# Block inverses of a gated delta rule on TensorE: the order of the 32x32 products, and the 64-block steps of two directions in one function

## Chip, cores and metric

The kernel runs on one core of a Trainium2 chip. The metric is device time in microseconds (us) of one execution. A profiled execution gives the rows below; its own time lies a little above the timed ones.

## What is computed

A two-layer encoder trunk over 256 tokens of width 1024. Each layer has a SwiGLU block, a mixer with two branches (a bidirectional gated delta rule and a multi-head latent attention), and a second SwiGLU block. The change lies in the delta rule of the mixer. Of the reference, this is the part:

```
unit = jnp.eye(C, dtype=f32) + lower                # lower: strictly triangular, C = 64
uw = lax.linalg.triangular_solve(unit, rhs, left_side=True, lower=True, unit_diagonal=True)
...
o_fwd = gated_delta_chunked(qh, kh, vh, g[:, :, 0], beta[:, :, 0])
o_bwd = flip(gated_delta_chunked(flip(qh), flip(kh), flip(vh), flip(g[:, :, 1]), flip(beta[:, :, 1])))
```

The kernel works on chunks of 128 tokens. Instead of solving, it forms the inverse of each 128x128 triangular matrix: two directions (d = 0, 1), two chunks (t) and four heads (h), so eight matrices n = (t, h) for each direction and layer.

## The kernel before

The inverse is built up by blocks. `gdn_base` makes the inverses of all 16x16 diagonal blocks by a recursion on GpSimd. Then come three doublings, each of two product steps: `inv0` and `inv1` go from 16 to 32, `inv2` and `inv3` from 32 to 64, `inv4` and `inv5` from 64 to 128. A step multiplies an off-diagonal block of `LA` (or a result `t1s` of the step before) by an inverse made so far (`XC`, `ZC`, its transpose, `x64` for the 64-blocks, `Z` for the whole). All of these are float32 in SBUF; one partition range of 32 or 64 rows holds one block row, so each product uses one 32x32 (or 64x64) place of the 128x128 array, given by the partitions that it reads and the partitions that it writes.

- `inv0(d)` and `inv1(d)` (lines 828 to 846) make 32 products of 32x32 each, in the four places on the diagonal of the array: the outer loop runs over the four places `Q`, the inner one over the eight matrices, so eight products in a row use one place. `inv0` is evicted by ScalarE (L834), `inv1` by VectorE (L841), which also transposes (L843) and copies into `Z` (L845).
- `inv2(d)` (L848 to L864) makes 16 products in two places, all eight of the first place and then all eight of the second; VectorE and ScalarE evict one half each (L857).
- `inv3(d)` (L866 to L881) makes 16 products `pu` in two places (L872) and then 8 products `px` in a third (L876).
- `inv4(d)` and `inv5(d)` (L883 to L896) make 8 products of 64x64 each, in one place for d = 0 and in another for d = 1.

The results go to PSUM tiles `gd`, of which there are two in turn. In the profile a float32 product is two pairs of a weight load and a matmul, so the 32 products of an `inv0` are x64 there. Below, a pair is one of these.

The steps are called in the order that the end of `mixer` lists (L1016 to L1037), but a scheduler then sets each engine's order by its own estimate of times, so that dense products of other parts (`qkv_group` L550, the gates and projections L141 to L143, the attention heads L644, L657, L674, L686) stand between the steps. Each engine works its list in order. Five bursts of 32x32 products result in each layer, each followed by other products: `inv0(0)`; `inv1(0)` with `inv0(1)`; `inv2(0)` with `inv1(1)`; `inv3(0)` with `inv2(1)`; and `inv3(1)`. They hold 64, 128, 96, 80 and 48 pairs.

Of the kernel before, what the change touches and what calls it, by code (L numbers as in the profile page):

```python
# [20 lines left out]
P = 128  # L21
# [16 lines left out]
def encoder_trunk(ctx: ExitStack, tc: tile.TileContext, x, positions, norm_ffn1, ffn1_w_gate, ffn1_w_up,  # L38
# [4 lines left out]
    V, A, G, T = nc.vector, nc.scalar, nc.gpsimd, nc.tensor  # L43
# [14 lines left out]
    def gdp():  # L58
        return psum.tile([P, 512], F32, tag="gd", name="gd", bufs=2)
# [358 lines left out]
    def mixer(l, next_gain):  # L418
# [7 lines left out]
        with tc.tile_pool(name="mix", bufs=1) as mp:  # L426
            def t2(tag, bufs, shape=(P, NH, P)):
                return mp.tile(list(shape), F32, tag=tag, name=tag, bufs=bufs)

            def g2(shape=(P, NH, P)):  # L430
                return t2("g2", 4, shape)
# [262 lines left out]
            LA, Z, egc, cs = {}, {}, {}, {}  # L694
# [21 lines left out]
            def gdn_nv(nk_):  # L716
                for t in range(NT):
                    pv = gdp()
                    for h in range(NH):
                        T.transpose(out=pv[:, h * P:(h + 1) * P], in_=vT[h // 2][:, h % 2, t * P:(t + 1) * P],  # L720
                                    identity=ident)
                    V.tensor_tensor(out=nV[t], in0=ev4(pv), in1=bc(nk_[:, t, :]), op=ALU.mult)
# [43 lines left out]
            N8 = NT * NH  # L766
# [3 lines left out]
            def flat(ap):  # L770
                return ap.rearrange("p a b -> p (a b)")
# [39 lines left out]
            def ij(d, b, o0):  # L811
                fst, snd = slice(o0, o0 + b), slice(o0 + b, o0 + 2 * b)
                return (snd, fst) if d == 0 else (fst, snd)

            def blocks(ps, c0, b):
                return ps[:, c0:c0 + N8 * b].rearrange("p (n d) -> p n d", d=b)

            TH = [(t, h) for t in range(NT) for h in range(NH)]
            Q = [slice(q * 32, q * 32 + 32) for q in range(4)]

            t1s, x64 = {}, {}
# [5 lines left out]

            def inv0(d):
                pv = blocks(gdp(), 0, 32)
                for r in Q:  # L830
                    for n, (t, h) in enumerate(TH):
                        T.matmul(pv[r, n], lhsT=LA[d, t][r, h, 1, r], rhs=XC[r, d, n], start=True, stop=True)
                t1s[d] = t2("t1", 4, (P, N8, 32))
                A.copy(out=t1s[d], in_=pv)  # L834

            def inv1(d):
                pv = blocks(gdp(), 0, 32)
                for r in Q:
                    for n in range(N8):
                        T.matmul(pv[r, n], lhsT=ZC[r, d, n], rhs=t1s[d][r, n], start=True, stop=True)  # L840
                V.copy_predicated(out=XC[:, d], mask=(mlo if d == 0 else mup)[:, None, :].to_broadcast([P, N8, 32]),  # L841
                                  data=pv)
                V.transpose(out=flat(ZC[:, d]), in_=flat(XC[:, d]))  # L843
                for q, r in enumerate(Q):
                    (A.copy if q % 2 else V.tensor_copy)(  # L845
                        out=Z[d][r, :, :, r].rearrange("p t h a -> p (t h) a"), in_=ZC[r, d])

            def inv2(d):  # L848
                pv = blocks(gdp(), 0, 32)
                t1s[d] = t2("t1", 4, (P, N8, 32))  # L850
                for o0 in (0, 64):
                    I, J = ij(d, 32, o0)
                    for n, (t, h) in enumerate(TH):
                        T.matmul(pv[I, n], lhsT=LA[d, t][J, h, 1, I], rhs=XC[J, d, n], start=True, stop=True)
                for o0 in (0, 64):
                    I, J = ij(d, 32, o0)
                    (A.copy if o0 else V.tensor_copy)(out=t1s[d][I], in_=pv[I])  # L857

                x64[d] = g2((P, N8, 64))
                o = 64 * d  # L860
                G.memset(x64[d][o:o + 64], 0.0)
                for k in range(2):
                    G.tensor_copy(out=x64[d][o + 32 * k:o + 32 * k + 32, :, 32 * k:32 * k + 32],
                                  in_=XC[o + 32 * k:o + 32 * k + 32, d])  # L864

            def inv3(d):  # L866
                ps = gdp()
                pu, px = blocks(ps, 0, 32), blocks(ps, N8 * 32, 32)
                for o0 in (0, 64):
                    I, J = ij(d, 32, o0)  # L870
                    for n, (t, h) in enumerate(TH):
                        T.matmul(pu[J, n], lhsT=t1s[d][I, n], rhs=ZC[I, d, n], start=True, stop=True)  # L872
                o = 64 * d
                I, J = ij(d, 32, o)
                for n in range(N8):
                    T.matmul(px[I, n], lhsT=ZC[I, d, n], rhs=t1s[d][I, n], start=True, stop=True)  # L876
                A.copy(out=x64[d][I, :, J.start - o:J.stop - o], in_=px[I])
                for o0 in (0, 64):
                    I, J = ij(d, 32, o0)
                    (A.copy if o0 else V.tensor_copy)(  # L880
                        out=Z[d][J, :, :, I].rearrange("p t h a -> p (t h) a"), in_=pu[J])  # L881

            def inv4(d):  # L883
                I, J = ij(d, 64, 0)
                pv = blocks(gdp(), 0, 64)
                t1s[d] = g2((P, N8, 64))
                for n, (t, h) in enumerate(TH):
                    T.matmul(pv[I, n], lhsT=LA[d, t][J, h, 1, I], rhs=x64[d][J, n], start=True, stop=True)
                (A.copy if d else V.tensor_copy)(out=t1s[d][I], in_=pv[I])

            def inv5(d):
                I, J = ij(d, 64, 0)
                pv = blocks(gdp(), 0, 64)
                for n, (t, h) in enumerate(TH):
                    T.matmul(pv[J, n], lhsT=t1s[d][I, n], rhs=Z[d][I, t, h, I], start=True, stop=True)
                (A.copy if d else V.tensor_copy)(out=Z[d][J, :, :, I].rearrange("p t h a -> p (t h) a"), in_=pv[J])  # L896

            zz, qs = {}, {}

# [115 lines left out]
            dense(xh, xl, NKC, wl_, C_Z, 512, ev_z)  # L1015
            inv_zero()  # L1016
            inv0(0)
            inv1(0)
            inv0(1)
            inv2(0)  # L1020
            inv1(1)
            m1 = mla_dense(1)
            gb = [gate(C_G + D)]
            gb.append(gate(C_G + D + 512))
            inv3(0)
            at0(0)
            inv2(1)
            at0(1)
            inv4(0)
            inv3(1)  # L1030
            inv4(1)
            qkv_group(4)
            qkv_group(5)
            gdn_nv(nk_)
            inv5(0)
            at1 = mla_heads(*m1)
            inv5(1)  # L1037
            sts = {}
            sts[0] = gdn_first(0)
            at1(0)  # L1040
# [34 lines left out]
    for l in range(depth):  # L1075
        ffn(ffn1_w_gate[l], ffn1_w_up[l], ffn1_w_down[l], G_MX + 8 * l, mixer_consts if l == 0 else None)
        mixer(l, G_F2 + 8 * l)
        ffn(ffn2_w_gate[l], ffn2_w_up[l], ffn2_w_down[l], G_F1 + 8 * (l + 1) if l + 1 < depth else None)
# [26 lines left out]
```

## Time and profile before

| | us |
|---|---|
| median of three timed runs | 1253.03 (1252.57 to 1253.27) |
| the profiled execution's own time | 1257.24 |
| span of the profiled execution | 1255.5 |
| TensorE busy in it | 1225.0 |
| VectorE busy | 774.5 |
| ScalarE busy | 624.1 |
| GpSimd busy | 132.7 |

The span runs from the first to the last instruction; about 1.7 us of the execution lie around it. The mixers' inverses lie at about 312 to 366 us in the first layer and 932 to 986 us in the second. In rows, PE is TensorE's matmuls, PEld its weight loads, DVE is VectorE, ACT ScalarE, POOL GpSimd, SP the engine that issues DMAs; L832 is line 832 of the kernel. Ends of matmuls are modelled, and overlap with the next starts, so what a piece takes on the path is read from its start to the next piece's start.

### The profile page before, as it was taken

Reading aid. Unit: us, or ns where it says so; the run is one execution under the profiler, and the core shown is the slowest. Engines: PE = TensorE matmul, PEld = TensorE weight load, DVE = VectorE, ACT = ScalarE, POOL = GpSimd, SP = SyncE. Lnnn points to the kernel's source line nnn. Section 1 sums busy time; section 2 is a strip of 40 time slices with the busy share of each in tenths; the row PEclk is TensorE's granted clock in tenths of the full one; section 3 lists DMA queues with packets and bytes.
Section 4 is the critical chain, followed back from the end, with each engine's and each line's share of the span. In section 5 each row is a group of like instructions: output and inputs, shape, how many; then the busy total and the mean of one; then the engine's idle time right before and its main releaser. Section 6 shows DMA issues by size and latency. Waiting matters only on the chain.

```text
span 1255.5 us, 17613 instructions
## 1 busy us (share of the span) xinstructions
PE 1225.0 (98%) x7064; PEld 1036.0 (83%) x7064; DVE 774.5 (62%) x1127; ACT 624.1 (50%) x911; POOL 132.7 (11%) x238
## 2 busy tenths in 40 slices
PE   8999999899999999999999999998999999999997
PEld 6888889777988888888888888897778788888886
DVE  5655557986757665555555554588876576555554
ACT  6554446556445455453454444465554455544443
POOL 1000001445001000000000000015540000000010
PEclk9999999999899999999999999998999999999999
DMA  7564555435232555555555555543452235565652
GB/s 266 176 198 149 204 185 158 154 120 168 69 101 81 173 183 175 194 168 196 192 183 187 182 169 207 178 147 121 144 162 75 68 134 185 168 201 169 200 185 84
DMA packets 114576, 202.70 MB, mean 161 GB/s; under 512 B 4107, under 2 KB 30399, under 8 KB 114495
## 3 DMA queue, kind: packets, MB, share of 16 engines
q1 hardware_dynamic: 114031, 200.52, 49.1%
q8 instruction: 55, 0.90, 0.3%
q10 hardware_dynamic: 464, 1.06, 0.2%
q14 instruction: 26, 0.21, 0.0%
HBM read 200.52 MB, written 1.05 MB: 161 GB/s over the span
## 4 chain that ended last, share of the span: by engine, by line
PE 88%; DVE 4%; POOL 4%; issue 1%; ACT 1%; DMA 0%; POOLq 0%; SPq 0%; ACTq 0%
PE acc L141 24%; PE acc L142 23%; PE acc L143 23%; PE acc L550 4%; PE ms L191 2%; DVE wlo L131 2%; POOL bt L798 1%; PE ms L686 1%; PE ms L657 1%; POOL t L800 1%; PE gd L141 1%; PE gd L142 1%; PE gd L143 1%; PE gd L927 1%; DVE cv L566 1%
## 5 line engine op out<-in xcount | busy, mean ns | idle before, releaser
L131 DVE TENSOR_TENSOR wlo<-raw,whi 128x1024 fp32r<-128x1024 f32 (+3 forms) x388 | 471.4, 1218 | 364.2 <-ACT whi L130 362.0
L130 ACT CAST whi<-raw 128x1024 fp32r<-128x1024 f32 (+3 forms) x388 | 399.7, 1033 | 429.4 <-PE acc L143 384.9
L142 PE MATMUL acc<-wlo,xh 128*128 128x512 f32 (+3 forms) x968 | 360.7, 374 | 0.0
L143 PE MATMUL acc<-whi,xl 128*128 128x512 f32 (+3 forms) x968 | 357.5, 372 | 0.0
L141 PE MATMUL acc<-whi,xh 128*128 128x512 f32 (+3 forms) x968 | 344.7, 375 | 0.1
L142 PEld LDWEIGHTS acc<-wlo,xh 128*128 128x128 f32 x968 | 182.4, 188 | 29.8 <-issue 0.4
L141 PEld LDWEIGHTS acc<-whi,xh 128*128 128x128 f32 x968 | 181.4, 188 | 30.3 <-ACT xh L115 0.8
L143 PEld LDWEIGHTS acc<-whi,xl 128*128 128x128 f32 x968 | 182.1, 188 | 29.2
L142 PE MATMUL acc<-wlo,hh 128*128 128x512 f32 x352 | 137.4, 390 | 0.0
L143 PE MATMUL acc<-whi,hl 128*128 128x512 f32 x352 | 137.1, 389 | 0.0
L141 PE MATMUL acc<-whi,hh 128*128 128x512 f32 x352 | 127.4, 392 | 0.0
L143 PEld LDWEIGHTS acc<-whi,hl 128*128 128x128 f32 x352 | 66.1, 188 | 13.8
L141 PEld LDWEIGHTS acc<-whi,hh 128*128 128x128 f32 x352 | 66.1, 188 | 13.7
L142 PEld LDWEIGHTS acc<-wlo,hh 128*128 128x128 f32 x352 | 66.1, 188 | 13.1
L141 PE MATMUL acc<-whi,fr 128*128 128x512 f32 (+1 forms) x152 | 60.7, 406 | 9.2 <-DVE pre L558 7.9
L142 PE MATMUL acc<-wlo,fr 128*128 128x512 f32 (+1 forms) x152 | 60.8, 402 | 0.0
L143 PE MATMUL acc<-whi,fr 128*128 128x512 f32 (+1 forms) x152 | 58.0, 399 | 2.4 <-DVE fr L116 2.4
L550 PE MATMUL acc<-xl,whi 128*128 128x256 f32 x192 | 56.9, 297 | 0.0
L550 PE MATMUL acc<-xh,whi 128*128 128x256 f32 x192 | 56.9, 298 | 0.0
L550 PE MATMUL acc<-xh,wlo 128*128 128x256 f32 x192 | 54.8, 296 | 0.0
L566 DVE SCALAR_TENSOR_TENSOR cv<-pre,ccol,cv 128x256 f32<-128x256 f32 x96 | 51.9, 572 | 0.0
L255 ACT ACTIVATE sil<-acc,rstd 128x512 f32<-128x512 f32 (+1 forms) x48 | 31.0, 654 | 29.5 <-PE acc L143 29.4
(299 smaller groups left out, 1277.7 us busy)
## 6 DMA issues: line engine op xcount, KB each, us to landing
raw<-in_ffn_w_up_dram SPq DMA_DIRECT2D x40, 1024.0 KB, 5.0
raw<-in_ffn_w_down_dram SPq DMA_DIRECT2D x40, 1024.0 KB, 5.0
raw<-in_ffn_w_gate_dram SPq DMA_DIRECT2D x38, 1024.0 KB, 5.0
raw<-in_w_in_dram SPq DMA_DIRECT2D x32, 1024.0 KB, 4.9
raw<-in_w_out_dram SPq DMA_DIRECT2D x8, 1024.0 KB, 4.9
raw<-in_ffn_w_gate_dram SPq DMA_DIRECT2D x12, 512.0 KB, 3.7
raw<-in_ffn_w_up_dram SPq DMA_DIRECT2D x8, 512.0 KB, 3.7
raw<-in_ffn_w_down_dram SPq DMA_DIRECT2D x8, 512.0 KB, 3.3
```

The source lines that it names most:

```text
L130: A.copy(out=hi[:, :n * w], in_=raw[:, k0 * w:(k0 + n) * w])
L131: V.tensor_tensor(out=lo[:, :n * w], in0=raw[:, k0 * w:(k0 + n) * w], in1=hi[:, :n * w].bitcast(F32), op=ALU.subtract)
L141: T.matmul(ps[t][:, :n], lhsT=a1, rhs=w[0], start=start, stop=False)
L142: T.matmul(ps[t][:, :n], lhsT=a1, rhs=w[1], start=False, stop=False)
L143: T.matmul(ps[t][:, :n], lhsT=a2, rhs=w[0], start=False, stop=stop)
L191: T.transpose(out=pt[:, i * S + t * P:i * S + (t + 1) * P], in_=srcs[t][:, (j + i) * P:(j + i + 1) * P], identity=ident)
L255: A.activation(out=sil[t][:, :w], in_=ps, func=AF.Silu, scale=rstds[0][:, t:t + 1])
L550: T.matmul(pc[:, c].rearrange("p (t s) -> p t s", s=P), lhsT=w[:, cc], rhs=a, start=(i == 0), stop=(i == len(terms) - 1))
L566: V.scalar_tensor_tensor(out=cv[:, c], in0=pre[:, c, d:d + S], scalar=wc, in1=cv[:, c], op0=ALU.mult, op1=ALU.add)
L657: T.matmul(sc[:, t * S:(t + 1) * S], lhsT=qT[:, t * P:(t + 1) * P], rhs=kT, start=True, stop=True)
L686: T.matmul(po[r:r + MV, :S], lhsT=v[:, kk, h, :], rhs=prT[:, kk, :], start=(kk == 0), stop=(kk == NT - 1))
L798: G.tensor_tensor(out=tv, in0=M[:, b + 1:16, b:b + 1].to_broadcast([P, na, nb]), in1=Y[:, b:b + 1, 0:nb].to_broadcast([P, na, nb]), op=ALU ...
```

## The change

`inv0` and `inv1` swap their loops: for each matrix, the four places in turn. `inv2` does so with its two places. `inv3` makes, for each matrix, the two `pu` products and then the `px` product. `inv4` and `inv5` lose their argument: one call makes both directions, direction by direction for each matrix, into two `gd` tiles taken at once, and is called after `inv3(1)`, and after `gdn_nv`, respectively. No product, copy or DMA is added or dropped.

```
             def inv0(d):
                 pv = blocks(gdp(), 0, 32)
-                for r in Q:
-                    for n, (t, h) in enumerate(TH):
+                for n, (t, h) in enumerate(TH):
+                    for r in Q:
                         T.matmul(pv[r, n], lhsT=LA[d, t][r, h, 1, r], rhs=XC[r, d, n], start=True, stop=True)
...
             def inv1(d):
-                for r in Q:
-                    for n in range(N8):
+                for n in range(N8):
+                    for r in Q:
                         T.matmul(pv[r, n], lhsT=ZC[r, d, n], rhs=t1s[d][r, n], start=True, stop=True)
...
             def inv2(d):
-                for o0 in (0, 64):
-                    I, J = ij(d, 32, o0)
-                    for n, (t, h) in enumerate(TH):
+                for n, (t, h) in enumerate(TH):
+                    for o0 in (0, 64):
+                        I, J = ij(d, 32, o0)
                         T.matmul(pv[I, n], lhsT=LA[d, t][J, h, 1, I], rhs=XC[J, d, n], start=True, stop=True)
...
             def inv3(d):
-                for o0 in (0, 64):
-                    I, J = ij(d, 32, o0)
-                    for n, (t, h) in enumerate(TH):
+                o = 64 * d
+                for n in range(N8):
+                    for o0 in (0, 64):
+                        I, J = ij(d, 32, o0)
                         T.matmul(pu[J, n], lhsT=t1s[d][I, n], rhs=ZC[I, d, n], start=True, stop=True)
-                o = 64 * d
-                I, J = ij(d, 32, o)
-                for n in range(N8):
+                    I, J = ij(d, 32, o)
                     T.matmul(px[I, n], lhsT=ZC[I, d, n], rhs=t1s[d][I, n], start=True, stop=True)
...
+            def inv4():
+                pvs = [blocks(gdp(), 0, 64) for _ in range(2)]
+                for d in range(2):
+                    t1s[d] = g2((P, N8, 64))
                 for n, (t, h) in enumerate(TH):
+                    for d in range(2):
+                        I, J = ij(d, 64, 0)
+                        T.matmul(pvs[d][I, n], lhsT=LA[d, t][J, h, 1, I], rhs=x64[d][J, n], start=True, stop=True)
+                for d in range(2):
+                    I, J = ij(d, 64, 0)
+                    (A.copy if d else V.tensor_copy)(out=t1s[d][I], in_=pvs[d][I])
...
-            inv4(0)
             inv3(1)
-            inv4(1)
+            inv4()
             qkv_group(4)
             qkv_group(5)
             gdn_nv(nk_)
-            inv5(0)
+            inv5()
             at1 = mla_heads(*m1)
-            inv5(1)
```

`inv5` is rewritten as `inv4` is.

The first place is TensorE's list at `inv3(0)` in the first layer, as the difference of the two programs. `t_2665` is `t1s[0]`; an x behind a row counts equal rows; L873 and L875 are the products that were L872 and L876.

```order
-L644 MATMUL ms<-ident,m_2727 96x128
-L872 MATMUL gd<-ZC,t_2665 32x32 x16
-L876 MATMUL gd<-t_2665,ZC 32x32 x8
+L644 MATMUL ms<-ident,m_2727 96x128 x2
+L873 MATMUL gd<-ZC,t_2665 32x32 x2
+L875 MATMUL gd<-t_2665,ZC 32x32
+L873 MATMUL gd<-ZC,t_2665 32x32 x2
+L875 MATMUL gd<-t_2665,ZC 32x32
```

The 24 products now go round three places, one product in each; one attention transpose (L644) more stands ahead of them. At `inv0`, `inv1` and `inv2` the two lists read alike, since a row doesn't say which place a product uses; the same products stand there in the new loop order.

The second place is TensorE's list around `inv4` of direction 0 in the first layer, before; `LA_1661` is `LA[0]`, `LA_1665` is `LA[1]`, `t_3020` is `t1s[1]`.

```order
L644 MATMUL ms<-ident,m_2728 96x128 x3
L888 MATMUL gd<-g_2684,LA_1661 64x64 x8
L872 MATMUL gd<-ZC,t_3020 32x32 x16
L876 MATMUL gd<-t_3020,ZC 32x32 x8
L644 MATMUL ms<-ident,m_2728 96x128
L657 MATMUL ms<-qk 128x256 x2
```

The direction 0 half of the 64-block step stood ahead of `inv3(1)`. The same place after the change, from the last rows of `inv3(1)` on:

```order
L873 MATMUL gd<-ZC,t_3020 32x32 x2
L875 MATMUL gd<-t_3020,ZC 32x32
L889 MATMUL gd<-g_2684,LA_1661 64x64 x8
L657 MATMUL ms<-qk 128x256 x2
L143 MATMUL acc<-whi,xl 128x512
L141 MATMUL acc<-whi,xh 128x512
```

It now stands behind `inv3(1)`. Direction 1 of the step stands where it stood, 18 dense products and the two L657 further on:

```order
L141 MATMUL acc<-whi,xh 128x512
L142 MATMUL acc<-wlo,xh 128x512
L889 MATMUL gd<-g_3039,LA_1665 64x64 x8
L720 MATMUL gd<-ident,ysb_1656 128x128 x4
L674 MATMUL ms<-ident,pr 128x128
```

So the scheduler keeps the two directions of `inv4` apart, in two runs of eight; the two runs of `inv5` are apart too, with the products between them that stood there before. The second layer has the same differences, and no other product of TensorE's list has moved.

## Rows read from the trace of the kernel before

**Rows 1.** The page: TensorE's share, and the chain that ended last, by engine.

```profile
PE 1225.0 (98%) x7064; PEld 1036.0 (83%) x7064; DVE 774.5 (62%) x1127; ACT 624.1 (50%) x911; POOL 132.7 (11%) x238
PE 88%; DVE 4%; POOL 4%; issue 1%; ACT 1%; DMA 0%; POOLq 0%; SPq 0%; ACTq 0%
```

**Rows 2.** Windows over both layers' inverses: length, each engine's busy us, PEclk (granted TensorE clock), DMA.

```profile
312.00:370.00 58.00, 57.14 (x701) 49.74 (x701) 38.81 (x80) 27.55 (x55) 3.10 (x7) 0.94 0.26 85
932.00:990.00 58.00, 56.58 (x707) 48.71 (x706) 40.10 (x82) 27.77 (x55) 3.39 (x8) 0.97 0.28 90
```

**Rows 3.** TensorE's waits from 312 to 372 us: us in total, times, longest.

```profile
PE ms L674 <- DVE pr L669: 1.4, 1, 1.4
```

**Rows 4.** Chain of work in order of time, first layer: start, us, what.

```profile
315.88 1.84 PE gd L832 x64
...
319.78 1.54 PE acc L550 x13
321.32 1.74 PE gd L840 x61
...
324.79 3.84 PE acc L550 x18
328.63 0.93 PE gd L854 x29
...
331.28 0.59 PE ms L674 x4
331.87 3.54 PE acc L550 x17
...
335.51 0.93 PE gd L872 x29
...
337.75 1.01 PE ms L686 x4
...
346.06 0.93 PE gd L872 x29
347.08 0.41 PE gd L876 x13
347.49 0.24 PE ms L644
```

**Rows 5.** TensorE's groups by form: count, then busy us and mean ns of one.

```profile
L832 PE MATMUL gd<-XC,LA 32*32 32x32 f32 x256 | 7.6, 192 | 0.0
```

**Rows 6.** TensorE's timeline where `pu` ends and `px` begins: start, us, instruction.

```profile
336.25 0.21 PE L876 MATMUL gd<-t,ZC 32*32 32x32 f32 x1
336.28 0.19 PE L872 MATMUL gd<-ZC,t 32*32 32x32 f32 x1
336.31 0.19 PE L876 MATMUL gd<-t,ZC 32*32 32x32 f32 x1
336.31 0.19 PE L872 MATMUL gd<-ZC,t 32*32 32x32 f32 x1
```

**Rows 7.** The same view: eight pairs in one full-width place, eight pairs round four places.

```profile
377.20 1.06 PE L917 MATMUL gd<-g,g 128*128 128x128 f32 x8
378.18 0.42 PE L583 MATMUL gd<-cv,ones 128*32 128x128 f32 x8
```

**Rows 8.** A window just behind a burst, columns as in Rows 2.

```profile
325.00:328.40 3.40, 3.40 (x18) 3.40 (x17) 1.97 (x6) 1.63 (x4) 0.19 (x2) 0.50 0.00 0
```

**Rows 9.** Chain in order of time, second layer.

```profile
945.72 3.72 PE acc L550 x18
...
952.76 2.04 PE acc L550 x17
```

**Rows 10.** VectorE's timeline beside the second burst; brackets: idle before, and what ended it.

```profile
319.82 0.69 DVE L659 TENSOR_REDUCE mxs<-ms 128x2 f32<-128x512 f32 x1 [0.72 <-PE ms L657]
...
323.20 0.44 DVE L841 COPY_PREDICATED XC<-mlo,gd 128x256 f32<-128x256 uint8 x1 [0.64 <-PE gd L840]
...
325.19 0.60 DVE L669 TENSOR_SCALAR pr<-pr,rs 128x256 f32<-128x256 f32 x2
```

More of the change, by code (lines that the diff above doesn't have):

```diff
@@ L881, in inv3, with inv5 @@
                         out=Z[d][J, :, :, I].rearrange("p t h a -> p (t h) a"), in_=pu[J])
[L883 to L886, printed above, removed]
+            def inv4():
+                pvs = [blocks(gdp(), 0, 64) for _ in range(2)]
+                for d in range(2):
+                    t1s[d] = g2((P, N8, 64))
                 for n, (t, h) in enumerate(TH):
[L888 to L893, printed above, removed]
-                for n, (t, h) in enumerate(TH):
-                    T.matmul(pv[J, n], lhsT=t1s[d][I, n], rhs=Z[d][I, t, h, I], start=True, stop=True)
-                (A.copy if d else V.tensor_copy)(out=Z[d][J, :, :, I].rearrange("p t h a -> p (t h) a"), in_=pv[J])
+                    for d in range(2):
[4 more added lines that the diff above has]
+                    (A.copy if d else V.tensor_copy)(out=t1s[d][I], in_=pvs[d][I])
+            def inv5():
+                pvs = [blocks(gdp(), 0, 64) for _ in range(2)]
+                for n, (t, h) in enumerate(TH):
+                    for d in range(2):
+                        I, J = ij(d, 64, 0)
+                        T.matmul(pvs[d][J, n], lhsT=t1s[d][I, n], rhs=Z[d][I, t, h, I], start=True, stop=True)
+                for d in range(2):
+                    I, J = ij(d, 64, 0)
+                    (A.copy if d else V.tensor_copy)(out=Z[d][J, :, :, I].rearrange("p t h a -> p (t h) a"),
+                                                     in_=pvs[d][J])
             zz, qs = {}, {}
```

## The prediction

> **What bounds the kernel now.** I read the page first: TensorE is busy for 98% of the span and holds 88% of the chain that ended last [rows 1]. Then the windows over the two stretches with the inverses, 58 us each: TensorE is busy for 57.1 and 56.6 of them, VectorE, the next, for 38.8 and 40.1 [rows 2], and in the first stretch TensorE waits once, for 1.4 us, on VectorE [rows 3]; that wait ends before the first burst begins. So time taken out of TensorE's list here shortens the kernel, unless a copy between two steps then comes too late. Third, the chain in order of time shows what TensorE does in these stretches: bursts of 32x32 products, and dense products between them [rows 4].
>
> Two things in it are dear. **The bursts:** from start to next start they take 1.84 us (315.88 to 317.72), 3.47 (321.32 to 324.79), 2.65 (328.63 to 331.28), 2.24 (335.51 to 337.75) and 1.43 (346.06 to 347.49), 11.63 us for 416 pairs in a layer [rows 4]. The second layer has the same ones: the four `inv0` together take 7.6 us, 1.9 each with the last pair's end [rows 5]. **The clock:** behind the second burst 18 dense products take 3.84 us, 0.213 each, and behind the third 17 take 3.54, 0.208 each; ahead of them 13 took 1.54, 0.118 each [rows 4]. In the window of the first of these the granted clock is 0.50, the 1.2 GHz level instead of 2.4 [rows 8]. In the second layer 18 take 3.72 us behind its second burst, but 17 behind its third take 2.04, 0.120 each [rows 9]. The mean clock of the two stretches, 0.94 and 0.97, agrees with two such dips of some 3.4 us and one [rows 2].
>
> **What a change of place does.** Within one place the pairs start 32 ns apart: 13 of them take 0.41 us [rows 4]. Sixteen pairs in each of four places, one place after the other, would be 4 x 16 x 32 ns = 2.05 us, yet the burst takes 1.84 with the hand-over to the next piece, some 0.1. The missing 0.3 us are at the three changes of place. [Rows 6] show one, from `pu` to `px` in the same PSUM tile: pairs of both places start in turn, at 336.25, .28, .31 and .31, so the new place runs while the last few pairs of the old one still do, each at its own pace. Its first step is longer, 0.06 us (336.25 to 336.31). So places work side by side, but only the next few pairs in the list are looked at; eight products in a row in one place leave the other three empty. That is what the new loop order removes. The nearest row of a list that goes round is L583: eight pairs over four places take 0.42 us, where eight in one full-width place take 1.06 [rows 7].
>
> **The change, part by part.** *Loop order of `inv0` to `inv3`.* If four places run side by side, a burst takes as long as the fullest place: 16 pairs are 0.51 us, 32 are 1.02, plus 0.02 for the longer first step and 0.1 for the hand-over. The bursts become 0.63, 1.14, 1.14 (two steps of 16 pairs a place), 1.14 and 0.63, 4.68 us, which would save 6.95 us a layer. That needs a pair every 8 ns. At the other end, what [rows 6] show over a few pairs is two places at a time, 16 ns a pair: 64, 128, 96, 80 and 48 pairs plus hand-overs are 1.12, 2.15, 1.64, 1.38 and 0.87, 7.16 us, 4.47 saved a layer. L583 is nearest in kind (it too goes round four places with two pairs in each) and speaks for the fast end, but it holds eight pairs, and nothing shows that TensorE can be fed 128 pairs at 8 ns. I take 10 ns: 0.74, 1.38, 1.14, 1.14 and 0.63, 5.03 us; 6.6 saved a layer, **13.2 us** in both. Bounds: 8.9 and 13.9.
>
> *The clock dips.* The clock fell after TensorE had done 32x32 products for 3.47 us, in both layers, and once after 2.65 us; after the first, fourth and fifth bursts (1.84, 2.24, 1.43 us) it didn't, nor after the third of the second layer. The longest burst is now 1.38 us at 10 ns a pair and 2.15 even at 16, below every burst that a dip followed, so I expect no dip. That gives back 3.84 - 18 x 0.119 = 1.70, 3.54 - 17 x 0.119 = 1.52 and 3.72 - 2.14 = 1.58 us, with 0.08 of a slow start of the burst behind the last: **4.9 us**. Bounds: 0, if they stay, and 4.9.
>
> *The copies between the steps.* No copy is added, but the covers shrink with TensorE's time. The closest is at L674 (331.28), whose input VectorE makes at 325.19 + 0.60 = 325.8 [rows 4, 10]. VectorE's own list moves up by its two waits on TensorE, 0.72 and 0.64 us, to 324.4, and no further, since it is full there [rows 10]. TensorE gets there at 331.28 - 1.1 - 2.1 - 1.7 - 1.5 = 324.9. So the cover holds by half a microsecond, and every later cover (the copies of `inv2` and `inv3`, the conversions of the next weights) is of the same small size where VectorE queues behind its own work. I allow **1 us** lost over both layers; bounds 0 and 3.
>
> *`inv4` and `inv5`.* The list of the changed kernel keeps the two directions apart, so no pair of these steps overlaps with the other direction's, and they cost what they cost. `inv4` of direction 0 now stands behind `inv3(1)`, 1.4 us later by today's burst; who waits for it is VectorE's copy of the result, which `inv5` needs only two or three dozen dense products further down the list. The two `gd` tiles taken at once hold nobody up: the list behind is that of before, and the copies that free them were done long ago. Nothing, both ways.
>
> **Sum:** 13.2 + 4.9 - 1.0 = 17.1 us off. The profiled execution's own time is 1257.2 us for a span of 1255.5, and would become 1240.1; it stands 4.2 above the median, so against the median of 1253.0 I forecast **1236 us**. What comes behind keeps the gain: TensorE bounds the rest [rows 1].
>
> **Rivals.** *Fed too slowly.* Two places at a time, or a supply of pairs that runs dry: 1253.0 - 8.9 - 4.9 + 1 = 1240.2. For it: [rows 6] show no more than two at once, and no row shows a long run. Against it: L583.
>
> *The dips stay.* The places are busier but for less time, and the clock may fall all the same: 1253.0 - 13.2 + 1 = 1240.8, or 1245.1 with the slow feed. For it: the trace has no burst of this kind; against it: bursts of up to 2.24 us without a dip [rows 4].
>
> *One product at a time.* If a small product had a price on TensorE as a whole, whatever its place, the order would change nothing: 416 pairs at 27 ns a pair are what there is, and the time stays 1253. The overlap in [rows 6] speaks against it, pairs of two places starting within 10 ns of each other and 32 ns apart in one place. The Trainium skill, TensorEngine Tiling (Array Packing), Instruction Overhead, has such a rule against this change: each matmul costs about 60 cycles however few its columns, and one should not take the tiling factor from a dimension that is already small. By that rule the time is this rival's. The same page, Restrictions and Gotchas, says that different row tiles cannot work on one PSUM bank at the same time, and all places of a step write one tile here; the trace disagrees where the partitions written differ, since `pu` and `px` in [rows 6] share a tile and overlap.
>
> *Slower: every change of place costs its first step.* If a place that is left and taken up again starts with the long first step, 0.06 us instead of 0.03, and the places don't overlap when each holds only one product, then a product costs 0.06 + 0.03 instead of 0.054: 208 products x 0.03 us = 6.4 us a layer, 12.9 in both, and longer bursts keep the dips: 1266. It decides as soon as a product costs more than 0.054 us, the present mean. [Rows 7] speak against it: L583 changes place after each product and is faster.
>
> **How the numbers follow.** The forecast, 1233.5 to 1238: 0.57. Fed too slowly, 1238 to 1242: 0.22. The dips stay, wholly or in part, 1240 to 1245: 0.08. One product at a time, 1250.5 to 1253.3: 0.09. Slower, 1258 to 1268: 0.04. The range 1233 to 1243 holds the first two and half of the third, 0.83. A measurement of this kernel can tell about 0.2%, 2.5 us, from no change: faster by more than that 0.87 plus a little of the fourth, 0.88; within it 0.08; slower 0.04.
>
> **What would show it.** In the changed kernel's trace: the pieces of L832 and L840 take some 0.6 to 0.8 us for 64 pairs instead of 1.74 to 1.84; the starts of neighbouring pairs lie 5 to 16 ns apart all through; granted clock of 1.00 in the windows behind the second and third bursts, with L550 at 0.12 us a product; `inv4` and `inv5` as long as before. New waits of TensorE of over 0.5 us at L674, L854 or L872 would show that the copies became the bound. The prediction is wrong if the bursts keep over 25 ns a pair, or if the dips move elsewhere.

## The result, and the profile after

The changed kernel takes 1241.27 us (1240.15 to 1241.65), the kernel before beside it 1253.15 (1252.57 to 1254.88): a ratio of 0.990, 95% interval 0.988 to 0.992. The forecast was 1236, with a range of 1233 to 1243. The profiled execution's own time is 1241.41 us for a span of 1239.7; that of before was 1257.24 for 1255.5.

The chain of work of the changed kernel in order of time, first layer (start, us, what), answers to [rows 4]. L832 and L840 are `inv0` and `inv1`, L854 `inv2`, L873 and L875 `inv3`, L889 `inv4`.

```profile
317.95 0.68 PE gd L832 x50
318.64 1.01 PE ms L686 x4
...
322.26 0.65 PE gd L840 x48
322.91 0.59 PE gd L832 x35
323.50 2.33 PE acc L550 x18
325.83 0.53 PE gd L854 x26
...
327.02 0.59 PE ms L674 x4
327.61 2.03 PE acc L550 x17
329.64 0.22 PE ms L644 x2
329.86 0.15 PE gd L873 x2
...
330.99 1.01 PE ms L686 x4
...
338.25 0.15 PE gd L873 x2
...
338.88 1.07 PE gd L889 x16
339.95 1.06 PE ms L657 x4
```

From start to next start the five bursts now take 0.69, 1.24, 1.19, 1.13 and 0.63 us: 4.88 instead of 11.63. Behind the second burst 18 L550 take 2.33 us and behind the third 17 take 2.03, 0.13 and 0.12 each, where they took 3.84 and 3.54. The windows over both layers' inverses and over the stretches behind the second and third bursts (columns as in [rows 2]) say why:

```profile
312.00:370.00 58.00, 56.82 (x761) 47.62 (x761) 42.88 (x87) 29.67 (x59) 4.42 (x11) 1.00 0.29 95
932.00:990.00 58.00, 57.11 (x713) 47.05 (x713) 39.26 (x90) 29.34 (x62) 6.14 (x10) 1.00 0.25 85
...
323.50:326.90 3.40, 3.40 (x115) 3.27 (x114) 3.32 (x11) 1.88 (x6) 1.19 (x4) 1.00 0.02 5
327.60:331.00 3.40, 3.40 (x101) 3.17 (x100) 2.81 (x7) 2.65 (x5) 0.87 (x2) 1.00 0.00 0
```

The granted clock is 1.00 where [rows 8] had 0.50, and no dip is left in the 58 us. TensorE's waits over the whole span (us in total, times, longest), one of before and three of after, answer to [rows 3]:

```profile
PE gd L927 <- ACT g L919: 0.7, 2, 0.4
```

```profile
PE ms L674 <- DVE pr L669: 2.6, 2, 1.4
PE gd L934 <- ACT g L926: 0.8, 2, 0.4
PE acc L550 <- issue: 0.5, 1, 0.5
```

L674 waits no longer than before (2.9 there). L934 is the line that was L927, and it waits for the same copy as before, once a layer for 0.4 us, behind the inverses; in the window of [rows 3] it is missing only because it lies at 379 us there. New is one thing, in the second layer: 0.5 us in which TensorE waits for nothing that the profile shows. In the chain:

```profile
933.83 1.62 PE acc L550 x12
935.45 0.52 issue
935.97 0.98 PE acc L550 x6
```

**Where the 15.8 us between the two profiled executions lie.** The first product of `inv0(0)` starts at 317.95, and at 315.88 before [rows 4]: the changed kernel is 2.1 us late as the stretch begins. The dense products behind the last burst (L657) start at 339.95; before they started at 347.49 + 0.24 = 347.73 [rows 4]. So the first stretch gained 9.85 us. The same two starts of the second layer, before and after, show 7.6 us gained:

```profile
936.80 1.84 PE gd L832 x64
...
967.15 0.86 PE ms L657 x4
```

```profile
928.28 0.68 PE gd L832 x50
...
951.07 1.06 PE ms L657 x4
```

That is 17.4 in the two stretches: 6.75 + 6.83 = 13.6 from the bursts (11.63 and 11.70 before, 4.88 and 4.87 now), and 4.1 from the three dips, since the L550 that took 3.84, 3.54 and 3.72 us now take 2.33, 2.03 and 1.62 + 0.98 = 2.60; less the 0.5 of `issue`, and small pieces. The changed kernel also gains 0.5 us between and behind the two stretches. The 2.1 us that were lost ahead of them go with two dips that the other profile doesn't have, at 7.84 and 274.1 us: the same dense products are 0.9 us late behind the first, and 2.4 behind the second. Windows of the kernel after and of the kernel before over the same times:

```profile
7.84:11.25 3.41, 3.23 (x10) 2.77 (x11) 2.75 (x5) 3.41 (x10) 0.00 (x0) 0.50 0.86 273
274.10:277.40 3.30, 3.30 (x9) 2.62 (x8) 3.30 (x9) 1.33 (x4) 0.00 (x0) 0.50 0.11 8
```

```profile
7.84:11.25 3.41, 3.18 (x14) 2.21 (x15) 2.70 (x5) 3.41 (x10) 0.00 (x0) 1.00 0.89 294
274.10:277.40 3.30, 3.30 (x17) 2.86 (x16) 3.30 (x10) 0.91 (x3) 0.00 (x0) 1.00 0.26 38
```

No product that was changed stands there. The kernel after, profiled once more (below, 1239.10 us), has neither, and a kernel with the old loop order (the joint `inv4` and `inv5` alone, below) has one like the second: its granted clock is 0.50 from 273.1 to 276.4 us.

### The profile page after: what moved, and what is told of

The parts are those of the page before. It is cut to its first block, busy times and chain, and to the rows that moved or that the text cites. A ratio compares the mean times of both kernels' runs of the same rounds, so it can differ in the third digit from the quotient of the medians.

```text
span 1239.7 us, 17613 instructions
## 1 busy us (share of the span) xinstructions
PE 1208.9 (98%) x7064; PEld 1019.4 (82%) x7064; DVE 774.4 (62%) x1127; ACT 623.7 (50%) x911; POOL 132.3 (11%) x238
## 4 chain that ended last, share of the span: by engine, by line
PE 88%; DVE 4%; POOL 4%; issue 2%; ACT 1%; DMA 0%; SPq 0%; POOLq 0%; ACTq 0%
PE acc L141 24%; PE acc L142 24%; PE acc L143 24%; PE acc L550 4%; PE ms L191 2%; DVE wlo L131 1%; POOL bt L798 1%; PE ms L657 1%; PE ms L686 1%; POOL t L800 1%; PE gd L142 1%; PE gd L143 1%; PE gd L141 1%; PE gd L934 1%; DVE cv L566 1%
## 5 line engine op out<-in xcount | busy, mean ns | idle before, releaser
L131 DVE TENSOR_TENSOR wlo<-raw,whi 128x1024 fp32r<-128x1024 f32 (+3 forms) x388 | 471.1, 1217 | 361.3 <-ACT whi L130 358.6
L143 PEld LDWEIGHTS acc<-whi,hl 128*128 128x128 f32 x352 | 66.1, 188 | 13.7
L550 PE MATMUL acc<-xl,whi 128*128 128x256 f32 x192 | 55.1, 287 | 0.5 <-issue 0.5
L550 PE MATMUL acc<-xh,whi 128*128 128x256 f32 x192 | 55.0, 288 | 0.0
L550 PE MATMUL acc<-xh,wlo 128*128 128x256 f32 x192 | 52.6, 284 | 0.0
```

What stands on the lines that cost most here:

```text
L131: V.tensor_tensor(out=lo[:, :n * w], in0=raw[:, k0 * w:(k0 + n) * w], in1=hi[:, :n * w].bitcast(F32), op=ALU.subtract)
L143: T.matmul(ps[t][:, :n], lhsT=a2, rhs=w[0], start=False, stop=stop)
L550: T.matmul(pc[:, c].rearrange("p (t s) -> p t s", s=P), lhsT=w[:, cc], rhs=a, start=(i == 0), stop=(i == len(terms) - 1))
```

## The experiments

**The kernel before, again.** No edit.

> The kernel before, unchanged, to see how its clock dips vary. Theory 1, the dips are not the same in every execution, and the profile of before (1257.24 us against a median of 1253.15) held more of them than the timed ones: the new profile has another set of dips, its mean clock is 0.992 or more where it is quicker, and its own time lies near 1253 us. Theory 2, the dips behind the second and third bursts belong to the kernel and come each time: again three of them, at about 325, 332 and 946 us, and a profile of 1257 us; then the changed kernel lost 4 to 5 us somewhere that its profile must show.

1257.68 us (1253.17 to 1260.18), ratio 0.999 [0.998, 1.001]. Its profile again has dips behind the second and third bursts of the first layer and behind the second of the second layer. So the dips belong to this kernel, but its executions scatter over 8 us. Over the 46 executions of it that stood beside the experiments the time follows the granted clock, which each execution reports; the right column has the eight of the changed kernel:

| granted clock | before, mean us (executions) | after |
|---|---|---|
| 0.985 | 1261.0 (2) | |
| 0.986 | 1259.8 (9) | |
| 0.987 | 1258.8 (8) | |
| 0.988 | 1258.4 (8) | |
| 0.989 | 1257.8 (3) | |
| 0.990 | 1256.9 (8) | |
| 0.991 | | 1241.41, 1241.65 |
| 0.992 | 1254.5 (3) | 1241.13, 1242.12 |
| 0.993 | 1252.9 (3) | 1240.15, 1240.96 |
| 0.994 | 1252.9 (2) | 1240.27 |
| 0.995 | | 1239.10 |

One dip of 3.4 us at half clock is 1.7 / 1255 = 0.0014 of the mean clock, so three of them are the step from 0.993 to 0.989: by this the executions of before at 1253 have some three dips fewer than those at 1258. The median of 1253.03 goes with the first kind, the profile of 1257.24 with the second. The clock of an execution tells how much time it spent at half clock, not where; no execution at 1253 was profiled, so that the dips missing in it are the ones behind the bursts is likely, but not shown.

**The parts of the change.** The loop order of `inv0` to `inv3` without the joint `inv4` and `inv5`:

> The new loop order in inv0 to inv3 alone; inv4 and inv5 called for each direction as before. Theory: all of the gain is in the loop order, ratio to before 0.990 to 0.991 (1241 us), the same as the changed kernel within 0.1%. Rival: the merged 64-block steps hold a part of it or cost some; then this one differs from the changed kernel by more than 1 us.

and the joint `inv4` and `inv5` without the loop order:

> inv4 and inv5 merged as in the change, inv0 to inv3 in the old loop order. Theory: TensorE's list keeps the directions apart, so nothing changes: ratio 0.999 to 1.001, bursts of 1.84 to 3.47 us as before. Rival: the two gd tiles taken at once or the later place of inv4(0) cost or save over 1 us.

The first takes 1240.45 us (1238.71 to 1240.84), ratio 0.987 [0.983, 0.990]; the second 1257.43 (1252.96 to 1259.88), ratio 1.000 [0.998, 1.002]. Three dips of its profile lie behind bursts too, but not behind the same ones: behind the third of the first layer, and the second and third of the second. The loop order is all of the gain; `inv4` and `inv5`, written together but listed apart, are worth nothing.

Then the loop order in halves, each against the kernel before (of each pair of steps the lines of one are shown):

```
 inv0, inv1 alone:
-                for r in Q:
-                    for n in range(N8):
+                for n in range(N8):
+                    for r in Q:
 inv2, inv3 alone:
-                for o0 in (0, 64):
-                    for n, (t, h) in enumerate(TH):
+                for n, (t, h) in enumerate(TH):
+                    for o0 in (0, 64):
```

> The other half of the split: only inv0 and inv1 go round the four places; inv2 and inv3 as before. By the paces measured, their 512 pairs in both layers save 512 x 18 ns = 9.2 us, and the longest stretch with one place at work is 1.5 us (inv1(1) is short now, inv2(0) 0.9 us; inv2(1) and inv3(0) 2.2 us less the short hand-overs). With inv2 and inv3 alone going round the places the time was 1248.4, some 4.7 us under the least disturbed executions of before. If the two halves add up, this one is 12.5 - 4.7 = 7.8 to 9 us under those: 1244 to 1245.5 without half-clock windows behind the bursts. If the windows come with inv2 and inv3, which fill two places and then one, there are one or two of them, and the times lie at 1246 to 1249 with a clock below 0.992.

> Only inv2 and inv3 go round the places; inv0 and inv1 run one place after the other as before. A layer's bursts then take by the measured paces: 1.84 (64 pairs in one place after the other), 3.47 (128 pairs), 1.74 + 0.25 for the third, about 0.6 + 0.25 for the fourth and 0.6 for the fifth. Of the 6.6 us a layer, inv0 and inv1 hold some 256 pairs x (27 - 9) ns = 4.6 and inv2 and inv3 160 pairs x (27 - 13) ns = 2.1. So I expect 2 x 2.1 = 4 us less than the kernel before, and 9 us more than the changed one: 1249 to 1254 by the dips. If the dips follow a stretch of 3.5 us with one place at work, the one behind the second burst of each layer stays in some executions, and times spread by some 3 us; the one behind the third is gone. If the dips come from somewhere else, they may lie anywhere.

1245.66 us (1243.82 to 1248.6), ratio 0.989 [0.987, 0.991], and 1248.36 (1246.39 to 1251.05), ratio 0.994 [0.991, 0.996], the latter a little under the 1249 to 1254 expected. Medians of so few executions carry the dips; what doesn't is the time that the bursts hold on TensorE, from a burst's start to the start of the next other product, the five of a layer added up:

| kernel | layer 1, us | layer 2, us |
|---|---|---|
| before | 11.63 | 11.70 |
| `inv0`, `inv1` in turn | 7.19 | 7.17 |
| `inv2`, `inv3` in turn | 9.31 | 9.31 |
| all in turn (`inv4`, `inv5` as before) | 4.87 | 4.87 |
| the changed kernel | 4.88 | 4.87 |
| the changed kernel, `inv0`, `inv1` two places at a time | 6.11 | 6.11 |

The halves add up: 8.97 and 4.71 us, 13.7 together; I had put 9.2 and 4. In neither kernel's profile does a dip lie behind a burst, though the second burst of the latter is as long as before, in both layers (in the first, 320.50 to 323.97). The window behind it, columns as in [rows 2]:

```profile
324.00:327.40 3.40, 3.40 (x77) 3.27 (x78) 2.56 (x8) 1.81 (x4) 0.20 (x2) 1.00 0.00 0
```

So one burst of 3.5 us does not bring a dip by itself.

**Two places at a time.** The changed kernel, its `inv0` and `inv1` going round the first two places and then the other two:

```
-                for n in range(N8):
-                    for r in Q:
-                        T.matmul(pv[r, n], ...)
+                for half_ in (Q[:2], Q[2:]):
+                    for n in range(N8):
+                        for r in half_:
+                            T.matmul(pv[r, n], ...)
```

> The changed kernel, but inv0 and inv1 go round two places at a time (all eight matrices in the places 0 and 1, then in 2 and 3). If the fullest place sets the pace, these pairs start 16 ns apart on the mean: the burst of 64 takes 1.02 + 0.1 = 1.1 us instead of 0.68, and the two layers lose 8 x 0.44 = 3.5 us against the changed kernel (about 1244.8 us). If a supply of some 9 ns a pair sets it, whatever the places, the time stays at 1241.3.

1243.24 us (1241.01 to 1244.22), ratio 0.989 [0.986, 0.992]. The bursts take 2 x 1.2 = 2.5 us more than in the changed kernel (table above), not the 3.5 expected. Its chain has the 64 pairs of `inv0(0)` at 1.04 us to the next start:

```profile
317.32 1.04 PE gd L833 x62
318.36 1.01 PE ms L686 x4
```

From the first start of an `inv0(0)` to its last, with two places in turn a pair starts every 14.5 ns on the mean, with four every 8.9; with one place after the other it is 27, the changes of place included, and 32 within a place. A fixed supply of pairs at 9 ns would have left these bursts as they were. So it is the place that holds the most of the next few pairs that sets the pace.

**The changed kernel again.** No edit.

> The changed kernel as it is, beside the kernel before on the same chip, in more rounds. My theory: the order of the 32x32 products alone is worth about 6.6 us a layer, 13.2 in all, and the rest of the difference to the kernel before is half-clock windows, which lie behind its long bursts in some of its executions. Then the median is 1240 to 1242 and its times spread less than those of before (which spread from 1252.6 to 1261), and the difference to the executions of before that have the highest clock is 12 to 13 us. Rival: the dips belong to any execution, and the two kernels spread alike.

1240.62 us (1239.1 to 1242.12) against 1257.36 (1252.62 to 1259.63) for before in the same session, ratio 0.987 [0.985, 0.989]: 16.7 us by medians, 12.4 at equal clock (0.993 in the table). Its four executions scatter by 3 us, the eleven of before by 7.

**How long TensorE can be fed.** The changed kernel and the kernel before, each product of `inv0` and `inv1` made three times over (the line of the changed kernel's `inv1`):

```
-                for n in range(N8):
+                for n in [n for n in range(N8) for _ in range(3)]:
```

> The changed kernel with each product of inv0 and inv1 made three times over (the same result, written again). The second burst of a layer becomes a stretch of some 416 pairs of small products without a dense one, four places in turn: 3.7 us at 8.9 ns a pair, as long as the longest burst of the kernel before. The extra products are 512 pairs a layer; at 8.9 ns 4.6 us a layer, 9.1 in both: about 1250 without dips. If a half-clock window follows any stretch of 32x32 products of that length, one is behind the second burst in both layers and the time is 3 us more. If it takes a stretch in which only one place of the array is at work, there is none. If the pace of a pair holds over 416 pairs, the supply of instructions is not a limit at 9 ns.

> The kernel before with each product of inv0 and inv1 made three times over, one place after the other. Beside the same with places in turn, in which TensorE stood still for 2.1 to 2.7 us ten times in all, each time at the end of a 16384-byte block of its instructions, with the next block asked for at 0.3 us on either side of the halt. My theory: a block holds 128 pairs, which take 1.1 us at 8.9 ns and 3.4 us at 27 ns, and a block takes about 2.5 us from request to first use; so at 27 ns a pair no such halt of over 0.5 us comes. The extra products are 1024 pairs, 27.6 us: 1285 by the profile. Rival: the halts belong to the number of instructions in a stretch, whatever their pace, and there are as many of them; then it is some 20 us more. The half-clock windows: by the theory that they follow long stretches with one place at work, now one lies behind or in each of the longer bursts.

With places in turn the time is 1274.07 us (1272.32 to 1275.88), not 1250. TensorE stands still in the middle of the bursts. Its waits over the span (us in total, times, longest), the chain, and the timeline between two halts (start, us, instruction, count, and in brackets the idle time ahead):

```profile
PE gd L832 <- issue: 9.7, 4, 2.7
PE gd L840 <- issue: 3.1, 2, 1.9
...
PE gd L873 <- issue: 2.3, 1, 2.3
PE gd L854 <- issue: 2.2, 1, 2.2
```

```profile
328.42 2.19 issue
330.61 1.27 PE gd L832 x82
331.89 2.73 issue
334.62 0.59 PE gd L832 x22
```

```profile
330.61 1.27 PE L832 MATMUL gd<-XC,LA 32*32 32x32 f32 x128 [2.19 <-issue]
```

Between the two halts lie exactly 128 pairs in 1.27 us. In the DMA view of the second halt, 331 to 335 us in 40 slices, one packet of the instruction queue is all that moves, and it starts at 332.2:

```profile
GB/s 0 0 0 0 0 0 0 0 0 0 0 0 164 0 0 0 0 0 0 0 0 0 0 0 0 0 0 0 0 0 0 0 0 0 0 0 0 0 0 0
...
q8 instruction: 1, 0.02, 1.4%
```

TensorE goes on at 334.62, 2.4 us after the packet's start; at the eight halts it is 2.3 to 2.7. Over the run this queue carries 63 packets and 1.03 MB, 16.4 KB each, so a block of 16384 bytes holds 128 pairs, 256 instructions of 64 bytes. At 8.9 ns a pair a block lasts 1.1 us and the next needs 2.3 or more, so the supply runs dry in a long enough burst; the eight halts shown, of 1.2 to 2.7 us, are 17.3 us, most of the 24 by which the expectation was too low. The rest goes with the clock: the profile has 0.50 for 17 us of the first layer's inverses and 7 of the second's. The 0.5 us of `issue` in the changed kernel's second layer (935.45, before an L550, behind a burst of 128 pairs) is the same thing small: a packet of that queue starts at 933.61 there, and TensorE goes on 2.4 us later.

With one place after the other there is not one such halt in the same number of pairs: at 27 ns a block lasts 3.5 us. (The expectation's ten halts of 2.1 to 2.7 us are the eight above.) The rival (halts by number) falls. Yet the time is 1323.87 us, 39 above the expectation. TensorE waits 3.2 us more at L486, behind the first layer's inverses, and the mean granted clock is 0.962, against 0.990 in the profile of before: 1322 x 0.038 - 1255 x 0.010, some 37 us. Windows, columns as in [rows 2]:

```profile
331.70:369.20 37.50, 37.50 (x623) 35.77 (x620) 4.94 (x12) 5.12 (x12) 1.67 (x4) 0.50 0.01 2
```

```profile
991.00:1021.00 30.00, 30.00 (x517) 28.50 (x514) 4.80 (x12) 4.39 (x11) 1.82 (x4) 0.50 0.01 2
```

TensorE is busy all through, and granted 1.2 GHz instead of 2.4 for 37 and 30 us on end, beginning in its longest bursts of 32x32 products. A pair then takes 51 ns in one place (189 of `inv1` in 9.65 us). So in both layers of this kernel the half clock begins while one small place after the other is at work, with TensorE busy. Whether it is the one place or the length can't be told from the other kernel, whose granted clock falls too, since there TensorE also stands idle.

**The 64-block steps really in turn.** The changed kernel takes two `gd` tiles, and its scheduler lists the directions apart. Two kernels put both directions' results into one tile; in the first one ScalarE copy takes out both of `inv4`, in the second VectorE and ScalarE take a half each, as in the changed kernel:

```
             def inv4():
-                pvs = [blocks(gdp(), 0, 64) for _ in range(2)]
+                pv = blocks(gdp(), 0, 64)
...
-                        T.matmul(pvs[d][I, n], ...)
+                        T.matmul(pv[I, n], ...)
```

> The changed kernel, with the 64-block steps of both directions really made together: one gd tile holds both directions' results, one ScalarE copy evicts the first step, so TensorE's list has the two directions' products in turn. My theory: a place of 64x64 costs 58 ns a product pair whatever the other place does, as with the 32x32 places, so each of the four runs of a layer that now take 1.07 us apart becomes one of 1.07 for two: 2.1 us a layer, 4.3 in both, and 1237 against 1241. Rival one: products of 64 rows fill too much of what feeds the array, and the two directions take 2.1 us together as they do apart: 1241. Rival two: the joint copy waits for the later direction and TensorE waits for it: 1242 to 1243.

> The changed kernel with the two directions of the 64-block steps in one gd tile, but two tiles and two copies (VectorE, ScalarE) out of it, as in the changed kernel. In the run with one joint copy, both directions' products did run side by side (30 ns a pair, 58 in each place), and the inverses of a layer ended some 4 us earlier, yet the time rose by 6: the scheduler gave the rest of the mixer another order, in which VectorE converts weights between the steps of the gated normalisation behind the delta rule, and TensorE waits 3.2 us in each layer for its last product, at a place where it has no dense products left. In the list of this kernel two of those conversions stand behind the first half of the normalisation, not ahead. If that is the whole cause, the wait shrinks to about 1 us and the time is 1238 to 1241. Rival: the joint place itself costs (the direction that was ready first is held up for the second), and the time stays at 1245 to 1248.

The first takes 1246.99 us (1246.29 to 1250.06), ratio 0.993 [0.991, 0.995], slower than the change (1240.62 beside it) and not the 1237 expected; the second, in another session, **1235.15 us** (1234.44 to 1235.75), ratio 0.982 [0.980, 0.984], faster than both kernels. In both, the products of the two directions run side by side. The chain of the second, where one piece now holds what took two of 1.07 us:

```profile
341.18 1.07 PE gd L889 x30
...
348.72 1.08 PE gd L899 x32
```

In a layer the steps hold 2.40 us of TensorE instead of 4.29, 3.8 less in both, and the span differs from that of the kernel after, profiled again, by 1237.4 - 1233.4 = 4.0. Two smaller changes go against each other: no wait is left for the copy of L926, which took 0.7 us, and the `issue` before an L550 of the second layer takes 1.1 us instead of 0.4. What the first kernel lost lies behind the inverses, where the scheduler made another order. One of TensorE's waits, over the span, and VectorE's timeline there (start, us, instruction):

```profile
PE ms L486 <- DVE g L967: 6.3, 2, 3.2
```

```profile
391.80 1.13 DVE L967 SCALAR_TENSOR_TENSOR g<-g,fac,zsil 128x128 f32<-128x128 f32 x4
...
393.17 1.23 DVE L131 TENSOR_TENSOR wlo<-raw,whi 128x1024 fp32r<-128x1024 f32 x1 [0.16 <-ACT whi L130]
...
394.99 1.22 DVE L131 TENSOR_TENSOR wlo<-raw,whi 128x1024 fp32r<-128x1024 f32 x1
...
396.38 1.14 DVE L967 SCALAR_TENSOR_TENSOR g<-g,fac,zsil 128x128 f32<-128x128 f32 x4
```

Two conversions of weights (L131) stand between the halves of the gated normalisation (L967), and TensorE, which needs the second half at L486, has no dense product left: 3.2 us in each layer, with a dip of 3.4 us behind each wait. The second kernel's list has the same two lines at other times, and no such wait:

```profile
382.36 1.14 DVE L969 SCALAR_TENSOR_TENSOR g<-g,fac,zsil 128x128 f32<-128x128 f32 x4
383.42 2.35 DVE L131 TENSOR_TENSOR wlo<-raw,whi 128x1024 fp32r<-128x1024 f32 x2
...
388.54 1.14 DVE L969 SCALAR_TENSOR_TENSOR g<-g,fac,zsil 128x128 f32<-128x128 f32 x4
```

The rival, that the joint place itself costs, falls; but so does my figure of 1238 to 1241, which allowed a wait of 1 us that is not there.

## Why the prediction was right, and which step was mis-sized

- **The bursts: right.** 13.2 us forecast, 13.6 measured (11.63 and 11.70 to 4.88 and 4.87). The pace of 10 ns a pair was taken between bounds of 8 and 16; it is 8.9. The reading of [rows 6], that places run side by side and that only the next few pairs are looked at, holds: two places in turn gave 14.5 ns, four 8.9.
- **The dips: right in the profile, wrong in the sum.** All three vanished, though they gave back 4.1 us and not 4.9, as the 18 L550 behind the second burst take 0.13 us each in the first layer and 0.14 in the second, not 0.119. That the shorter bursts kept them away is not shown: with `inv2` and `inv3` alone in turn a burst of 3.5 us stood in each layer without a dip behind it. The profiled execution lands at 1241.4, near the 1240.1 worked out for it, with the two dips elsewhere against it. But the 4.9 us were then subtracted from a median of 1253.03 that, by its place in the table of clocks, didn't hold them. The 4.2 us by which the profiled execution stood above that median were a sign of it: about the price of its three dips. The sum against the median should have been 13.2 - 1 = 12.2, 1240.8; at equal clock 12.4 were measured. In later sessions, where the median of before was 1257 to 1260, the whole 17 came out: 16.7 in one. This is the mis-sized step, 4.9 of the 5.3 us by which 1236 was too low.
- **The copies: nothing lost.** 1 us was allowed. No cover at L674, L854 or L872 broke, and no wait for a copy is new. What is new is 0.5 us of instruction supply, which I had only as a rival.
- **`inv4` and `inv5`: right.** Their four runs in a layer still take 4.29 us, and alone they changed nothing.
- **The rivals.** *One product at a time* is out: the same 832 pairs of both layers take 9.8 us instead of 23.3, so a small product has no price on TensorE as a whole beyond 8.9 ns a pair. The Trainium skill, TensorEngine Tiling (Array Packing), Instruction Overhead, has 60 cycles for each matmul; the runs here show such a price within one place only, 27 to 32 ns a pair, and not for the array. *Slower* is out with it; its price was also mis-added, since 208 x 0.03 us are 6.2 and not 6.4. *The dips stay* is out for this kernel, in both of its profiles. *Fed too slowly* is true of bursts that go on past some 128 pairs, and the longest here is 128: 0.5 us of it is seen, in one layer. I had written that nothing showed that 128 pairs can be fed at 8 ns; at 8.9 they can, and not many more: the changed kernel with its products made three times over made 176 before its first halt.
- **What was luck.** 1241.27 lies outside the 1233.5 to 1238 that I gave to the forecast itself, and inside the 1238 to 1242 of *Fed too slowly*, which at 8.9 ns a pair is not what happened. The range held because it was made wide enough for a rival, not because the last subtraction was sound.

## What to carry to other kernels

Small products in different places of the array overlap much only if the list itself goes round the places: at a change of place only some three pairs of each ran side by side. Then the fullest place sets the pace, down to 8.9 ns a pair here, until the list uses up blocks of instructions, of 128 pairs each, faster than they come. Steps meant to run together need a list that has them in turn (here it took a shared result tile), and the order made must be read: two edits that differ in the copies out of that tile cost 6 us or gained 4 to 6 by what was listed elsewhere. And before a gain in clock is subtracted from a median, compare the profile's granted clock with those of the timed executions: a dip that they don't have can't be saved in them.

## What the runs showed of the hardware that I had not expected

- Instructions are a resource of TensorE: blocks of 16384 bytes, 128 weight load and matmul pairs, 2.3 to 2.7 us from the start of the block's packet to TensorE's going on. A list that uses a block in 1.1 us stands still for 1.2 to 2.7 us, eight times, and one that takes 3.5 us never does (the two kernels with products made three times over).
- The half clock can last: 37 and 30 us on end with TensorE busy all the time, when long bursts of 32x32 products in one place come close together. One burst of 3.5 us left the clock alone in the profile with only `inv2` and `inv3` in turn, and was followed by a dip in that of before. What decides between them stays open, and so does why the dips of the kernel before went away.
- Two 64x64 places at opposite corners run side by side as the 32x32 ones do: 58 ns a pair in each, 30 ns between starts on the mean, with results in one PSUM tile (the kernel of 1235.15 us).
